# Low products ahead of high ones in every second weight block of a wide product

## The chip, the cores and the metric

The kernel runs on one core of a Trainium2 chip. The metric is the device time of one execution in microseconds; the figure before is the median of three runs. TensorE (PE) multiplies into PSUM, VectorE (DVE) and ScalarE (ACT) split weights and evacuate PSUM, GpSimd (POOL) does little here, and SyncE (SP) issues nearly all loads.

## What is computed

Two transformer-like layers run over one sequence of 256 tokens with 2048 features. The first has an adaptive normalization, four kinds of attention and a gated feed-forward part; the second has banded attention, a recurrent time mix, a cross attention on a memory, and three gated products that are merged. What matters for this change is that nearly all work is products of an activation with a large weight matrix:

```python
def first_block(x, c, ...):
    mod = c_act @ ada_w[layer] + ada_b[layer]
    u = rms_norm(h, norm_mix_g[layer]) * (1.0 + sc1) + sh1
    h = h + g1 * hybrid_mixer(u, w_in[layer], ..., w_out[layer])
    u = rms_norm(h, norm_ffn_g[layer]) * (1.0 + sc2) + sh2
    h = h + g2 * swiglu(u, ffn_w_gate[layer], ffn_w_up[layer], ffn_w_down[layer])
    return rms_norm(h, final_norm_g)

def hybrid_layer(x, mem, ...):
    proj = h @ w_in
    ...
    merged = (jax.nn.sigmoid(ga) * (ya @ w_up_a)
              + jax.nn.sigmoid(gb) * (yb @ w_up_b)
              + jax.nn.sigmoid(gc) * (yc @ w_up_c))
    return x + merged @ w_o
```

## The kernel before

A product is computed in a split form: a weight W is cast to a high part Wh, and the low part is Wl = W - Wh; an activation tile X[k] holds its high part in columns 0 to 255 and its low part in columns 256 to 511. The method `piece` loads one weight block of 128 x 1024 with a DMA on SyncE's queue (L296), casts it on ScalarE (L298) and subtracts on VectorE (L299). There are three buffers each of W, Wh and Wl.

The method `unit_b` is the feature-major product (weights are the stationary operand). A unit makes two output tiles of 128 features in two PSUM banks (`pd`, four banks in all) and walks over the K input tiles in blocks of four k, so that a block has eight weight tiles. Where the product is wide (`self.narrow` is false), a block has eight high products, Wh times both halves of X[k], 512 columns, and then eight low products, Wl times the high half of X[k], 256 columns into the first half of the same bank. The sum of the two halves of a bank is made at the end by `total` (L228 copy on ScalarE, L229 addition on VectorE). K is 16 for most products (four blocks a unit), 8 for w_out (two blocks) and 22 for ffn_w_down (six blocks, the last a half one). `narrow` is true only in the first phase, `start`, whose products have another form. `unit_a` is the token-major product, where activations are stationary; it isn't touched. All matmuls are recorded by the helper `mm` (L194), so in the profile they are told apart by their tiles: pd<-s,Wh and pd<-s,Wl are the ones spoken of.

The products are in program order, with two things interleaved: `step` advances side tasks (attention heads, the scan) after each block, and `trickle` issues pieces of the ada_w product, which VectorE computes (L457). A scheduler then orders each engine's instructions by its own estimates; the accumulations of a bank may change places in it. Phases in the profiled execution: `start` to about 200 us, the first layer's mixer to 530, its output product w_out with the last heads to 615, ffn from 630 to about 1300, the second layer behind it. In the second half of w_out the evacuation also squares the new rows (L1097 on ScalarE) and adds the squares up (L1101 on VectorE); ffn begins with a normalization by that sum.

Of the kernel before, what the change touches and what calls it, by code (L numbers as in the profile page):

```python
# [151 lines left out]
class Build:  # L152
# [158 lines left out]
    def unit_b(self, X, w, segs, evacs, row0=0, full=False):  # L311


        nb = len(evacs)
        K = len(X)
        first, part = self.parts.pop((w, tuple(segs)), (0, None))
        if part is not None:
            evacs = [self.add_part(part[:, b * 256:b * 256 + 256], evacs[b]) for b in range(nb)]
        ps = [self.pd.tile([128, 512], F32, name="pd", tag="pd") for _ in range(nb)]
        kp = 1024 // (128 * nb)  # L320
        for k0 in range(first, K, kp):
            nk = min(kp, K - k0)
            if full:
                W = self.whole(w, row0, segs, k0, nk, 128 * nb)
            else:
                Wh, Wl = self.piece(w, row0, segs, k0, nk, 128 * nb)
            tiles = [(b, k0 + j, slice(b * 128, b * 128 + 128), j) for b in range(nb) for j in range(nk)]

            for b, k, c, j in tiles:
                if full:  # L330
                    self.mm(ps[b][:, :256], W[:, j, c], X[k], k == 0, k == K - 1)
                elif self.narrow:
                    self.mm(ps[b][:, :256], Wh[:, j, c], X[k][:, :256], k == first, False)
                    self.mm(ps[b][:, :256], Wh[:, j, c], X[k][:, 256:], False, False)
                else:
                    self.mm(ps[b], Wh[:, j, c], X[k], k == first, False)
            for b, k, c, j in () if full else tiles:
                self.mm(ps[b][:, :256], Wl[:, j, c], X[k][:, :256], False, k == K - 1)
            if k0 + nk == K:
                for b in range(nb):  # L340
                    evacs[b](ps[b])
            self.trickle(self.rate)
            self.step()
# [1512 lines left out]
```

## Time and profile before

| | before |
|---|---|
| median of 3 runs | 2491.7 us (2488.88 to 2492.43) |
| profiled execution | 2491.23 us |
| its span, first to last instruction | 2489.5 us |
| mean granted TensorE clock | 0.988 of full speed |
| TensorE busy | 2417.4 us, 97% |
| VectorE busy | 1748.2 us, 70% |
| ScalarE busy | 1254.9 us, 50% |
| DMA | 527.12 MB, mean 212 GB/s |

Busy times are those of one profiled execution. A matmul's end in the profile is modelled and its row overlaps the next one, so the pace of TensorE is read from starts. A row of the timeline merges equal instructions that follow each other on one engine; its duration runs from the first start to the last modelled end.

### The profile page before, as it was taken

How to read it: one execution, taken by the hardware profiler on the slowest of the kernel's cores; microseconds unless marked ns; L12 is line 12 of the kernel's file. 1: busy time of each engine (PE TensorE's matmuls, PEld its weight loads, DVE VectorE, ACT ScalarE, POOL GpSimd, SP SyncE). 2: the span in 40 equal slices, each digit the busy share in tenths (PEclk: the TensorE clock that was granted, in tenths of full speed). 3: DMA queues.
4: the chain of work that ended last, by engine and by line, in shares of the span. 5: the costliest groups of instructions: out<-in, count | busy, mean ns of one | idle time of the engine just before them, and what ended most of it. 6: DMA issues, size and time to landing. Idle time of an engine off the chain costs nothing.

```text
span 2489.5 us, 38757 instructions
## 1 busy us (share of the span) xinstructions
PE 2417.4 (97%) x14666; PEld 2064.1 (83%) x14666; DVE 1748.2 (70%) x3321; ACT 1254.9 (50%) x2134; POOL 55.5 (2%) x102
## 2 busy tenths in 40 slices
PE   7989999998899999999999999999999999999999
PEld 5668788776788888888888877888888888888888
DVE  6677777899667755555566787778986766666664
ACT  3035446774544444444455554566564645444543
POOL 0000000000000000000000002000110000000000
PEclk9999999999899999999999999999999999999999
DMA  9988778778588866666655655335553465666665
GB/s 332 363 328 290 230 275 289 253 251 284 161 270 285 279 185 190 193 188 187 189 184 185 216 176 178 112 115 162 163 156 124 148 191 186 188 192 187 186 231 167
DMA packets 161095, 527.12 MB, mean 212 GB/s; under 512 B 22878, under 2 KB 32892, under 8 KB 160780
## 3 DMA queue, kind: packets, MB, share of 16 engines
q1 hardware_dynamic: 156892, 515.98, 63.4%
q0 software_dynamic: 4016, 8.66, 1.1%
q8 instruction: 115, 1.88, 0.3%
q14 instruction: 72, 0.59, 0.1%
HBM read 516.17 MB, written 9.45 MB: 211 GB/s over the span
## 4 chain that ended last, share of the span: by engine, by line
PE 81%; DVE 9%; DMA 6%; ACT 2%; issue 2%; SPq 0%; DVEq 0%; ACTq 0%
PE pd L194 74%; PE ps L194 7%; DVE Wl L299 3%; DMA W<-in_w_in_dram 2%; DMA b<-in_ada_w_dram 1%; ACT Wh L298 1%; DVE b L457 1%; PE ps L198 1%; DMA W<-in_w_out_dram 1%; DMA s<-in_memt_dram 0%; DVE dt L229 0%; DMA Wl<-in_w_mem_kv_dram 0%; DMA s<-in_xt_dram 0%; DMA tab<-fd 0%; DVE b L1306 0%
## 5 line engine op out<-in xcount | busy, mean ns | idle before, releaser
L194 PE MATMUL pd<-s,Wh 128*128 128x512 f32 (+1 forms) x5648 | 1423.3, 393 | 25.4 <-ACT Wh L298 11.2
L299 DVE TENSOR_TENSOR Wl<-W,Wh 128x1024 fp32r<-128x1024 f32 (+1 forms) x738 | 889.1, 1206 | 548.1 <-ACT Wh L298 526.6
L298 ACT CAST Wh<-W 128x1024 fp32r<-128x1024 f32 (+1 forms) x738 | 763.2, 1035 | 883.2 <-PE pd L194 627.2
L194 PEld LDWEIGHTS pd<-s,Wh 128*128 128x128 f32 x5648 | 1008.1, 190 | 210.6 <-ACT Wh L298 15.0
L194 PEld LDWEIGHTS pd<-s,Wl 128*128 128x128 f32 x5536 | 764.5, 191 | 72.7 <-DVE Wl L299 9.3
L194 PE MATMUL pd<-s,Wl 128*128 128x256 f32 x5536 | 793.5, 286 | 11.0 <-DMA Wl<-in_w_mem_kv_dram 5.6
L457 DVE SCALAR_TENSOR_TENSOR b<-b,tq 128x1024 f32<-128x1024 f32 x192 | 233.5, 1220 | 51.0 <-DMA b<-in_ada_w_dram 50.3
L194 PE MATMUL pd<-Wh,s 128*128 128x512 f32 (+4 forms) x496 | 141.6, 373 | 0.0
L229 DVE TENSOR_TENSOR dt<-pd,dt 128x256 f32<-128x256 f32 x289 | 110.4, 416 | 11.2 <-ACT dt L228 10.7
L228 ACT COPY dt<-pd 128x256 f32<-128x256 f32 x289 | 94.9, 371 | 24.4 <-PE pd L194 22.4
L194 PEld LDWEIGHTS pd<-Wh,s 128*128 128x128 f32 x496 | 88.4, 189 | 20.5 <-issue 11.9
L194 PE MATMUL pd<-Wl,s 128*128 128x512 f32 (+4 forms) x264 | 96.3, 386 | 0.0
L194 PE MATMUL ps<-s 64*128 64x256 f32 (+7 forms) x356 | 65.0, 364 | 4.5 <-DVE s L1612 2.5
L194 PEld LDWEIGHTS pd<-Wl,s 128*128 128x128 f32 x264 | 49.8, 189 | 14.2 <-issue 10.2
L194 PEld LDWEIGHTS ps<-s 64*128 64x128 f32 (+4 forms) x356 | 43.6, 184 | 21.2 <-issue 6.6
L194 PE MATMUL ps<-q,con 128*128 128x256 f32 x132 | 40.4, 412 | 11.3 <-ACT q L1091 4.2
L214 DVE TENSOR_TENSOR s<-q,s 128x256 fp32r<-128x256 f32 x104 | 39.8, 420 | 7.2 <-ACT s L213 6.9
L629 ACT ACTIVATE e<-e,y 128x256 f32<-128x256 f32 x80 | 35.8, 449 | 17.9 <-DVE y L627 17.7
L194 PEld LDWEIGHTS ps<-q,con 128*128 128x128 f32 x132 | 23.4, 197 | 20.3 <-ACT q L1091 4.4
L213 ACT CAST s<-q 128x256 fp32r<-128x256 f32 x104 | 37.6, 403 | 3.7 <-DVE q L1727 1.9
L636 ACT ACTIVATE e<-e,y 128x256 f32<-128x256 f32 x88 | 33.7, 447 | 4.3 <-DVE y L673 3.1
L206 ACT ACT_TABLE_LOAD x25 | 32.1, 1283 | 0.4
(295 smaller groups left out, 1381.8 us busy)
## 6 DMA issues: line engine op xcount, KB each, us to landing
W<-in_w_in_dram SPq DMA_DIRECT2D x334, 512.0 KB, 3.7
b<-in_ada_w_dram SPq DMA_DIRECT2D x192, 512.0 KB, 5.2
W<-in_ffn_w_gate_dram SPq DMA_DIRECT2D x88, 512.0 KB, 3.9
W<-in_ffn_w_up_dram SPq DMA_DIRECT2D x88, 512.0 KB, 4.4
W<-in_ffn_w_down_dram SPq DMA_DIRECT2D x80, 512.0 KB, 3.5
W<-in_w_out_dram SPq DMA_DIRECT2D x32, 512.0 KB, 4.2
W<-in_w_o_dram SPq DMA_DIRECT2D x32, 512.0 KB, 3.7
W<-in_w_up_a_dram SPq DMA_DIRECT2D x16, 512.0 KB, 3.6
```

What stands on the lines that cost most here:

```text
L194: self.nc.tensor.matmul(out, lhsT, rhs, start=start, stop=stop)
L198: self.nc.tensor.transpose(out, in_, self.ident[p0:p0 + n, p0:p0 + n])
L206: self.nc.scalar.activation(out, x, AF.Abs_reciprocal_sqrt)
L213: self.nc.scalar.copy(out[:, :256], src)
L214: self.nc.vector.tensor_tensor(out[:, 256:], src, out[:, :256], op=OP.subtract)
L228: self.nc.scalar.copy(t, ps[:, 256:512])
L229: self.nc.vector.tensor_tensor(t, ps[:, :256], t, op=OP.add)
L298: nc.scalar.copy(Wh[:, :n], W[:, :n])
L299: nc.vector.tensor_tensor(Wl[:, :n], W[:, :n], Wh[:, :n], op=OP.subtract)
L457: nc.vector.scalar_tensor_tensor(W, W, 1.0, self.crow[half], op0=OP.mult, op1=OP.mult, accum_out=acc[:, k:k + 1])
L629: nc.scalar.activation(e[:, lo:hi], e[:, lo:hi], AF.Exp, bias=nm[:, a:a + 1], accum_out=sm[:, a:a + 1])
L636: self.nc.scalar.activation(e[:, lo:hi], e[:, lo:hi], AF.Copy, scale=f[:, a:a + 1])
```

## The change

In a wide unit, the blocks are counted from the first one; in every second of them (the second, the fourth and so on) the low products are recorded ahead of the high ones. The flag that ends an accumulation moves with the last product. The first block of a unit stays as it was, so the flag that starts an accumulation stays with a high product. The same products are made with the same operands. The program order of a unit with four blocks becomes high, low, low, high, high, low, low, high, and the next unit begins with high.

```diff
+            swap = (k0 - first) // kp % 2 == 1 and not full and not self.narrow
+            if swap:
+                for b, k, c, j in tiles:
+                    self.mm(ps[b][:, :256], Wl[:, j, c], X[k][:, :256], False, False)
             for b, k, c, j in tiles:
                 if full:
                     self.mm(ps[b][:, :256], W[:, j, c], X[k], k == 0, k == K - 1)
...
                 else:
-                    self.mm(ps[b], Wh[:, j, c], X[k], k == first, False)
-            for b, k, c, j in () if full else tiles:
+                    self.mm(ps[b], Wh[:, j, c], X[k], k == first, swap and k == K - 1)
+            for b, k, c, j in () if full or swap else tiles:
                 self.mm(ps[b][:, :256], Wl[:, j, c], X[k][:, :256], False, k == K - 1)
```

The scheduler makes other orders of it. On TensorE in the mixer, ahead of the side products 7x128 of the first attention heads, the difference of the two orders reads as follows (pd are the unit's banks, s the activation tiles, ps the side tasks' banks):

```order
 L194 MATMUL pd<-s,Wl 128x256 x8
 L194 MATMUL pd<-s,Wh 128x512 x8
-L194 MATMUL pd<-s,Wl 128x256 x8
-L194 MATMUL pd<-s,Wh 128x512 x8
-L194 MATMUL pd<-s,Wl 128x256 x8
-L194 MATMUL pd<-s,Wh 128x512 x8
-L194 MATMUL pd<-s,Wl 128x256 x5
+L194 MATMUL pd<-s,Wl 128x256 x16
+L194 MATMUL pd<-s,Wh 128x512 x14
 L194 MATMUL ps<-s,y 7x128
```

The runs of eight have become runs of 16, and the side products now cut a run of high products instead of a run of low ones.

On VectorE in the second half of w_out, before the change (Wl the split, dt the addition of a bank's halves, s_389 and its neighbours the updated rows, b2 the ada pieces, s_5516 the sum of squares):

```order
L299 TENSOR_TENSOR Wl_5726<-W_5724,Wh_5725 128x1024
L229 TENSOR_TENSOR dt_5707<-pd_5658,dt_5707 128x256
L229 TENSOR_TENSOR dt_5713<-pd_5659,dt_5713 128x256
L1076 SCALAR_TENSOR_TENSOR s_389<-dt_5707,mod_87,s_389 128x256
L1076 SCALAR_TENSOR_TENSOR s_389<-dt_5713,mod_87,s_389 128x256
L457 SCALAR_TENSOR_TENSOR b2_5746,y_5617<-b2_5746,tq_88 128x1024
L299 TENSOR_TENSOR Wl_5751<-W_5749,Wh_5750 128x1024
L1101 TENSOR_TENSOR s_5516<-s_5516,s_5711 128x512
L457 SCALAR_TENSOR_TENSOR b2_5783,y_5617<-b2_5783,tq_88 128x1024
L299 TENSOR_TENSOR Wl_5790<-W_5788,Wh_5789 128x1024
```

The same stretch of VectorE after the change (line numbers behind the edit are five higher):

```order
L299 TENSOR_TENSOR Wl_5726<-W_5724,Wh_5725 128x1024
L229 TENSOR_TENSOR dt_5707<-pd_5658,dt_5707 128x256
L462 SCALAR_TENSOR_TENSOR b2_5746,y_5617<-b2_5746,tq_88 128x1024
L1081 SCALAR_TENSOR_TENSOR s_389<-dt_5707,mod_87,s_389 128x256
L229 TENSOR_TENSOR dt_5713<-pd_5659,dt_5713 128x256
L299 TENSOR_TENSOR Wl_5751<-W_5749,Wh_5750 128x1024
L1081 SCALAR_TENSOR_TENSOR s_389<-dt_5713,mod_87,s_389 128x256
L462 SCALAR_TENSOR_TENSOR b2_5783,y_5617<-b2_5783,tq_88 128x1024
L1106 TENSOR_TENSOR s_5516<-s_5516,s_5711 128x512
L299 TENSOR_TENSOR Wl_5790<-W_5788,Wh_5789 128x1024
```

The second addition and update now stand behind an ada piece and on both sides of the next split, and the sum of squares stands one ada piece later.

On TensorE at the end of w_out, before the change (ps<-s,con are the products of the sum of squares):

```order
L194 MATMUL pd<-s,Wh 128x512 x16
L194 MATMUL pd<-s,Wl 128x256 x16
L194 MATMUL pd<-s,Wh 128x512 x8
L194 MATMUL pd<-s,Wl 128x256 x5
L194 MATMUL ps<-s,con 128x256 x2
L194 MATMUL pd<-s,Wl 128x256 x3
L194 MATMUL ps<-q,con 128x256 x2
```

The same place on TensorE after the change:

```order
L194 MATMUL pd<-s,Wl 128x256 x8
L194 MATMUL pd<-s,Wh 128x512 x8
L194 MATMUL pd<-s,Wl 128x256 x16
L194 MATMUL pd<-s,Wh 128x512 x8
L194 MATMUL ps<-s,con 128x256 x2
L194 MATMUL ps<-q,con 128x256 x2
```

The last weight block's high products now stand behind its low ones, and the side products have moved behind both.

## Rows read from the trace of the kernel before

**Rows 1.** The page's busy shares, then TensorE's groups by line and form.

```profile
PE 2417.4 (97%) x14666; PEld 2064.1 (83%) x14666; DVE 1748.2 (70%) x3321; ACT 1254.9 (50%) x2134; POOL 55.5 (2%) x102
...
L194 PE MATMUL pd<-s,Wh 128*128 128x512 f32 x5344 | 1372.2, 397 | 11.7 <-DVE s L214 10.3 <-DVE s L239 0.6 <-ACT Wh L298 0.3
L194 PE MATMUL pd<-s,Wl 128*128 128x256 f32 x5536 | 793.5, 286 | 11.0 <-DMA Wl<-in_w_mem_kv_dram 5.6 <-DVE Wl L299 5.4
```

**Rows 2.** Windows: length, busy time of each engine, granted clock, DMA, by stage.

```profile
530.00:650.00 120.00, 96.13 (x476) 77.31 (x476) 107.88 (x229) 71.37 (x140) 0.00 (x0) 0.89 0.69 230
650.00:1300.00 650.00, 650.00 (x3724) 571.70 (x3723) 401.03 (x537) 307.87 (x449) 0.00 (x0) 1.00 0.67 215
1300.00:2000.00 700.00, 689.22 (x4945) 588.70 (x4944) 539.30 (x1149) 391.23 (x660) 44.60 (x78) 1.00 0.51 158
```

**Rows 3.** Waits of TensorE for Wl: whole span, then 530 to 650 us.

```profile
PE pd L194 <- DVE Wl L299: 5.4, 8, 1.6
...
PE pd L194 <- DVE Wl L299: 4.8, 7, 1.6
```

**Rows 4.** Timeline of TensorE in ffn (start, duration, engine, line, operation, count).

```profile
1201.94 2.00 PE L194 MATMUL pd<-s,Wh 128*128 128x512 f32 x8
1203.79 1.11 PE L194 MATMUL pd<-s,Wl 128*128 128x256 f32 x8
1204.74 0.63 PE L194 MATMUL pd<-s,Wh 128*128 128x512 f32 x2
```

**Rows 5.** Timeline of TensorE at 551 us, a run of 16 high products.

```profile
551.60 3.82 PE L194 MATMUL pd<-s,Wh 128*128 128x512 f32 x16
```

**Rows 6.** Timeline of TensorE from 1204.43 us: the last four of a low run.

```profile
1204.26 0.64 PE L194 MATMUL pd<-s,Wl 128*128 128x256 f32 x4
```

**Rows 7.** Timeline in ffn: a split (VectorE) and the block that uses it.

```profile
1009.53 1.22 DVE L299 TENSOR_TENSOR Wl<-W,Wh 128x1024 fp32r<-128x1024 f32 x1 [1.29 <-ACT Wh L298]
...
1016.63 0.64 PE L194 MATMUL pd<-s,Wl 128*128 128x256 f32 x4
```

**Rows 8.** Timeline of TensorE with side work between runs, 1674 to 1678 us.

```profile
1674.63 1.20 PE L194 MATMUL pd<-s,Wl 128*128 128x256 f32 x8
1675.67 1.02 PE L194 MATMUL ps<-s,con 128*128 128x256 f32 x4
1676.34 2.19 PE L194 MATMUL pd<-s,Wh 128*128 128x512 f32 x8
1678.37 0.88 PE L194 MATMUL pd<-s,Wl 128*128 128x256 f32 x6
```

**Rows 9.** Timeline in the second half of w_out, one unit.

```profile
598.79 1.22 DVE L299 TENSOR_TENSOR Wl<-W,Wh 128x1024 fp32r<-128x1024 f32 x1
...
600.06 1.21 PE L194 MATMUL pd<-s,Wl 128*128 128x256 f32 x8 [0.37 <-DVE Wl L299]
...
600.84 0.85 ACT L228 COPY dt<-pd 128x256 f32<-128x256 f32 x2 [0.17 <-PE pd L194]
...
602.21 0.75 DVE L229 TENSOR_TENSOR dt<-pd,dt 128x256 f32<-128x256 f32 x2
...
602.87 0.87 DVE L1076 SCALAR_TENSOR_TENSOR s<-dt,mod,s 128x256 f32<-128x256 f32 x2
...
603.73 1.22 DVE L457 SCALAR_TENSOR_TENSOR b<-b,tq 128x1024 f32<-128x1024 f32 x1
...
605.36 0.72 ACT L1097 ACTIVATE s<-s 128x256 f32<-128x256 f32 x2
...
606.11 0.69 DVE L1101 TENSOR_TENSOR s<-s 128x512 f32<-128x512 f32 x1 [1.08 <-ACT s L1097]
606.72 1.22 DVE L299 TENSOR_TENSOR Wl<-W,Wh 128x1024 fp32r<-128x1024 f32 x1
```

**Rows 10.** Timeline at the end of w_out.

```profile
612.92 1.22 DVE L299 TENSOR_TENSOR Wl<-W,Wh 128x1024 fp32r<-128x1024 f32 x1
...
615.58 0.70 PE L194 MATMUL pd<-s,Wl 128*128 128x256 f32 x3
```

## The prediction

> **What bounds the kernel now.** I read first the page's busy shares and the groups by line. TensorE is busy for 97% of the span, and the wide high products (5344 matmuls of 512 columns in wide blocks, written H here) and the low products (256 columns, L) are its two largest groups [rows 1]. A busy TensorE is modelled, so I read the stages next. From 650 to 1300 us TensorE has no idle time at all, from 1300 to 2000 it lacks 11 us of 700, but from 530 to 650 it is busy for 96 of 120 us while VectorE is busy for 108 [rows 2]. So there are two regimes. Where TensorE issues without a gap, the time is the sum of the distances from one matmul's start to the next. From 530 to 650 the loop of weight load, split and evacuation sets the pace, and seven of TensorE's waits there, 4.8 us, end with the low half Wl of a weight block [rows 3].
>
> The pace inside a regular block is in the timeline of 1202 to 1205 us: eight H take 1.85 us from the first start to the first L, eight L 0.95 us to the next H, a block 2.80 us [rows 4]. In one place the scheduler already put two blocks' H side by side: a run of 16 H shows 3.82 us against 2.00 us for a run of 8. Both figures end with the same modelled last matmul, so the second eight cost 1.82 us, 0.03 less than the eight that follow an L [rows 4, 5]. For L I compare the halves of a run: starts at 1203.79, 1204.26 and 1204.74, so 0.47 us for the first four and 0.48 for the last four [rows 4, 6]. The first L after an H are a little cheap, the first H after an L a little dear; neither is a pause that a join would remove whole.
>
> **The change part by part.** *Count of matmuls, weight loads, splits, DMAs:* the same, no cost. 337 of the 676 wide blocks stand the other way round.
>
> *H runs joined.* Counted over the two instruction orders, an H run follows directly on an L 608 times before and 349 times after. In 530 to 650 us, where TensorE isn't the bound, the count goes from 22 to 25; elsewhere 262 such places go. At 0.03 us each: -7.9 us. The rows are rounded to 0.01, so 0.02 to 0.04, -5.2 to -10.5 us.
>
> *L runs joined.* An L run follows directly on an H 666 times before, 344 after; 321 of the lost places lie outside 530 to 650 us. Each takes the cheap first four with it: 0.01 us each, +3.2 us (bounds 0 and 0.02 by rounding, 0 to +6.4). Net of the two: **-4.7 us**; with all bounds against each other -10.5 to +1.2.
>
> These joins are pace, and nothing else is late there: from 650 to 1300 us the first L of a block starts at 1016.63 us while its Wl was ready at 1009.53 + 1.22 = 1010.75, 5.9 us earlier [rows 7]. In a swapped block L starts 1.85 us sooner, and the Wh buffer of a swapped block is freed 0.95 us later, because its H stand last; the later cast and subtraction behind that eat into the same cushion, and it stays above 3 us. On SyncE's queue the weight DMAs wait for the subtraction that frees W, which moves by the same 0.95 us; the loads of ada_w between them keep their order. VectorE and ScalarE lose nothing there.
>
> *Side work between the runs.* Attention and scan matmuls cut runs about as often as before (179 runs of side work before, 181 after), but at other points: H after side work 118 to 87 times, L after it 32 to 65 times. The rows price one entry: eight H after side work take 1676.34 to 1678.37, 2.03 us against 1.85, so +0.18; eight L take 1674.63 to 1675.67, 1.04 against 0.95, so +0.09 [rows 4, 8]. That would be 31 x 0.18 less 33 x 0.09 = -2.6 us; but the side matmul ahead of an L may pay its part, which these rows don't separate, and the number of cuts is equal, so the other end is 0. I take **-1.0 us**, nearer to none.
>
> *Waits on Wl outside 530 to 650 us.* Only 0.6 us of the 5.4 us that TensorE waits for Wl lies there [rows 3]. A swapped block near scan or attention work may find Wl late by up to 1.85 us. Bounds: 0, and as much again as the 4.8 us of the other stretch; I take **+0.5 us**, since the plain blocks there hardly wait.
>
> *530 to 650 us, product w_out.* A unit has two blocks, and the second is now L before H. In the timeline Wl of a second block is ready at 600.01, its L run, the copies and additions follow, the squares stand at 605.36, their sum at 606.11, and the next unit's Wl starts at 606.72, 7.93 us after the one at 598.79 [rows 9]. Before, H was done while TensorE waited; after, it stands between Wl and the evacuation. The chain from Wl to the next such Wl is then L 0.95 + H 1.85 + copy 0.43 (half of the pair) + additions 0.75 + updates 0.87 + squares 0.72 + sum 0.69 + split 1.22 = 7.48 us without hand-overs: just under the loop of 7.93 us that is there now. The order on VectorE fills the later wait with an ada product ahead of the additions. So I take **+1.0 us** for some units that miss; bounds 0 and 12 (below). The last unit has nothing behind it to hide in: its Wl is ready at 612.92 + 1.22 = 614.14, and its last L ends at 615.58 + 0.70 = 616.28, because four side products stand between; that is 2.1 us, and after the change it is 0.95 us of L and a run of eight H, 2.00 us with its end, 2.95 us in all [rows 4, 10]. ffn's normalization waits for that: **+0.8 us**.
>
> *Sum:* -4.7 - 1.0 + 0.5 + 1.0 + 0.8 = **-3.4 us**. Against the profiled execution (2491.2 us, its span 2489.5) that is 2487.8 us; the profiled execution is 0.5 us under the median of 2491.7.
>
> **The rivals.** *The order of matmuls is free.* If the 0.03 us of rows 4 and 5 belongs to that one place, joining brings nothing: -1.0 + 2.3 gives 2492.5 us. For it: the rows show one clean run of 16 H and none of 16 L at full pace. Against it: H and L pace differ by position in the same run. The Trainium skill's page "TensorE: Matmul & The Clock Gate", section "Back-to-back issue gap", gives a warm distance of N / 2.4 + 2.5 ns, which depends on the columns alone; by it a block would be 8 x 216 + 8 x 109 ns = 2.6 us in any order, and the change would do nothing. The trace doesn't agree on the level (2.80 us) and shows 1.85 and 1.82 us for the same eight matmuls.
>
> *More comes of it.* With 0.04 us per H join, nothing lost at L, the full price of the side entries and no new waits: -10.5 - 2.6 = -13 us, 2478 us; the middle of this case is 2482.
>
> *Slower: w_out's loop takes the H in.* If an ada product (1.22 us) stands ahead of the additions and the squares follow it, the chain is 8.7 us against 7.93, 0.8 us more in each of 16 units, +12.4 us: 2491.2 - 5.7 + 0.5 + 0.8 + 12.4 = 2499 us. It decides from about 0.6 us per unit, where it outweighs the 3.4 + 1.0 us and another 5. For it: VectorE's 90% in that stretch. Against it: the additions there could already start late, behind a whole product and a split.
>
> **How the numbers follow.** Forecast 0.45 (2485 to 2490), free order 0.22 (2490 to 2494), more 0.19 (below 2485), slower loop 0.14 (above 2494). Below 2481.5 lies about half of the third, above 2496.5 some two thirds of the fourth: the range is 2481.5 to 2496.5. A measurement of this kernel tells about 0.2%, 5 us, from no change. Faster by more (below 2486.7): the third and a third of the forecast, 0.35. Slower by more: 0.09 of the fourth and a little for what I don't see, 0.11. The same: 0.54. So the likeliest outcome is a small gain at the edge of what can be told.
>
> **What would show it.** In the ffn stage a pair of blocks should take 2 x 2.80 less 0.02 us, a run of 16 H 3.82 us and a run of 16 L 0.96 us more than one of 8. From 650 to 1300 us TensorE should stay without idle time. From 530 to 650 us the stretch should last within 3 us of before; if it grows by 10, the slower rival holds. The prediction is wrong in its main term if a pair of blocks isn't shorter, or is shorter by over 0.05 us.

## The result and the profile after

The changed kernel takes 2511.2 us (median of 5 runs, 2506.7 to 2519.3), against 2491.7 us before: a ratio of 1.0085, 95% interval 1.0071 to 1.01. It is slower by 19.5 us. The prediction had a gain, 2487.8 us, with a range from 2481.5 to 2496.5: wrong in sign and in size. The profiled execution took 2508.21 us (span 2506.4).

The page after the change, busy shares and chain, then TensorE's two large groups by line and form (busy, mean ns, idle time ahead of them and its releasers); they answer to [rows 1]:

```profile
PE 2419.7 (97%) x14666; PEld 2065.0 (82%) x14666; DVE 1778.4 (71%) x3321; ACT 1260.3 (50%) x2134; POOL 55.6 (2%) x102
...
PE 66%; issue 11%; DMA 10%; DVE 9%; ACT 3%; POOL 1%; SPq 0%; DVEq 0%; ACTq 0%; POOLq 0%
...
L194 PE MATMUL pd<-s,Wh 128*128 128x512 f32 x5344 | 1316.0, 395 | 23.1 <-ACT Wh L298 13.2 <-DVE s L214 9.7 <-DVE s L239 0.2
L194 PE MATMUL pd<-s,Wl 128*128 128x256 f32 x5536 | 754.9, 287 | 17.7 <-DVE Wl L299 12.7 <-DVE q L568 2.9 <-ACT s L213 1.8
```

The joins worked: the high products are busy for 56 us less and the low ones for 39 us less, but a busy time counts the modelled ends, which fall away when runs are joined, so this is no gain in time; TensorE's busy time as a whole is 2.3 us longer. What is new is idle time: 13.2 us ahead of the high products that ended with the cast to Wh, 0.3 before, and 12.7 us ahead of the low ones that ended with Wl, 5.4 before.

The windows of the changed kernel by stage (length, busy time of each engine, granted clock, DMA share, GB/s), against [rows 2]. The stage from 650 to 1300 us is cut in three; the last two rows are the kernel before in two of the three parts:

```profile
530.00:650.00 120.00, 91.37 (x475) 73.91 (x474) 110.67 (x233) 70.71 (x139) 0.00 (x0) 0.93 0.68 227
650.00:740.00 90.00, 90.00 (x518) 79.50 (x517) 59.44 (x79) 45.26 (x67) 0.00 (x0) 1.00 0.73 234
740.00:905.00 165.00, 156.54 (x872) 133.35 (x871) 115.08 (x171) 72.61 (x110) 0.00 (x0) 1.00 0.74 252
905.00:1300.00 395.00, 395.00 (x2276) 349.24 (x2275) 226.24 (x280) 187.08 (x267) 0.00 (x0) 1.00 0.62 190
1300.00:2000.00 700.00, 688.44 (x4926) 587.00 (x4925) 538.03 (x1136) 388.98 (x653) 44.70 (x78) 1.00 0.51 157
...
740.00:905.00 165.00, 165.00 (x948) 145.26 (x947) 120.28 (x174) 77.78 (x114) 0.00 (x0) 1.00 0.77 261
905.00:1300.00 395.00, 395.00 (x2263) 347.26 (x2262) 220.08 (x281) 186.03 (x270) 0.00 (x0) 1.00 0.61 189
```

From 740 to 905 us TensorE now lacks 8.5 us, in a stretch where it had lacked none. That is the gate and up products of ffn's first half, and it is the part of ffn beside which most of the last 32 pieces of ada_w run: their products start from 700 to 889 us, 25 of them behind 740.

To place the loss I compare the start of the n-th high product in two traces; the number of such products is the same in every version, so the difference is how far one kernel lags behind the other. In a swapped block the high products come last, so this reading moves by up to 1 us with the place in a unit; where the order of runs differs, as at 527 us, it jumps. The changed kernel lags by 1.7 us at 422 us (time of before), 4.3 to 7.0 at 527, 4.6 at 685, 4.8 at 741, **16.9 at 908**, 15.7 at 1244 and 18.3 at the end, where the two spans differ by 16.9. Twelve of the 18 us arise between 741 and 908, some 3 to 5 between 422 and 685 (where runs scatter by as much), and in the rest of ffn the lag shrinks.

What the engines wait for from 740 to 905 us (us in total, times, longest), first before, then after:

```profile
ACT Wh L298 <- PE pd L194: 66.1, 42, 2.1
DVE Wl L299 <- ACT Wh L298: 34.1, 37, 2.2
...
DVE b L457 <- DMA b<-in_ada_w_dram: 8.0, 10, 1.5
```

```profile
ACT q L1141 <- DVE dt L229: 30.6, 7, 5.0
DVE b L462 <- DMA b<-in_ada_w_dram: 28.4, 13, 2.6
ACT Wh L298 <- DMA W<-in_ffn_w_gate_dram: 22.4, 11, 2.8
...
ACT Wh L298 <- DMA W<-in_ffn_w_up_dram: 14.4, 6, 2.6
```

Before, the cast (L298) waited for TensorE to free a Wh buffer: the supply of weights was ahead of TensorE. After, it waits for weight loads, and VectorE for loads of ada_w: the supply is behind. What reaches TensorE of this, in the same stretch of the changed kernel:

```profile
PE pd L194 <- ACT Wh L298: 4.5, 5, 1.2
...
PE pd L194 <- DVE Wl L299: 3.7, 7, 0.6
```

**The round.** The timeline of the changed kernel shows how that closes on itself (start, duration, engine, line, operation, in brackets the idle time ahead and its end):

```profile
784.64 0.42 SPq L201 DMA_DIRECT2D b<-in_ada_w_dram  x1
...
790.84 1.23 DVE L462 SCALAR_TENSOR_TENSOR b<-b,tq 128x1024 f32<-128x1024 f32 x1 [2.38 <-DMA b<-in_ada_w_dram]
...
792.00 0.42 DVE L229 TENSOR_TENSOR dt<-pd,dt 128x256 f32<-128x256 f32 x1
...
792.45 0.42 ACT L1141 ACTIVATE q<-dt 128x256 f32<-128x256 f32 x1 [4.70 <-DVE dt L229]
...
792.77 1.03 ACT L298 CAST Wh<-W 128x1024 fp32r<-128x1024 f32 x1
...
793.83 2.49 DVE L299 TENSOR_TENSOR Wl<-W,Wh 128x1024 fp32r<-128x1024 f32 x2 [0.82 <-ACT Wh L298]
...
793.86 2.14 PE L194 MATMUL pd<-s,Wh 128*128 128x512 f32 x8 [0.96 <-ACT Wh L298]
...
795.09 1.59 SPq L296 DMA_DIRECT2D W<-in_ffn_w_gate_dram  x2
...
796.73 0.43 SPq L201 DMA_DIRECT2D b<-in_ada_w_dram  x1
```

A load of ada_w leaves SyncE at 784.64, behind weight loads; it lands 6.2 us later, and the ada product starts at 790.84. Behind it VectorE has the addition of the gate, for which ScalarE's silu waits (4.70 us); behind the silu stands the cast, behind the cast the two subtractions Wl, and only these free two W buffers, so that SyncE can issue the two weight loads at 795.09 and, behind them, a load of ada_w at 796.73. Another one had left at 788.87, so a round holds two pieces. One round is 796.73 - 784.64 = 12.09 us and feeds four blocks, for which TensorE needs 4 x 2.79 = 11.16 us. Over 24 pieces in the middle of the stretch (718 to 852 us before, 724 to 869 after) two pieces take 12.13 us, against 11.16 before. The lag grows from 741 to 867 us (time of before), which is 126 / 11.16 = 11.3 rounds; 11.3 x 0.97 = 11 us of the 11.9 that it grows by.

The same piece of work in the kernel before:

```profile
779.18 1.23 DVE L457 SCALAR_TENSOR_TENSOR b<-b,tq 128x1024 f32<-128x1024 f32 x1 [0.30 <-DMA b<-in_ada_w_dram]
...
780.75 1.23 DVE L299 TENSOR_TENSOR Wl<-W,Wh 128x1024 fp32r<-128x1024 f32 x1
...
781.89 0.75 DVE L229 TENSOR_TENSOR dt<-pd,dt 128x256 f32<-128x256 f32 x2
...
782.00 3.32 SPq L296 DMA_DIRECT2D W<-in_ffn_w_gate_dram  x2
782.35 0.42 ACT L1136 ACTIVATE q<-dt 128x256 f32<-128x256 f32 x1 [1.43 <-DVE dt L229]
```

Here a subtraction stands between product and additions, and a W buffer is free (load at 782.00) before the silu has run. The scheduler had changed VectorE's order with the swap: from product, split, addition, addition to product, addition, addition, split, split. SyncE's order, two weight loads and one of ada_w in turn, is the same in both.

### The profile page after: what moved, and what is told of

Read it like the earlier page. It is cut to its first block, busy times and chain, and to the rows that moved or that the text cites. A ratio compares the mean times of both kernels' runs of the same rounds, so it can differ in the third digit from the quotient of the medians.

```text
span 2506.4 us, 38715 instructions
## 1 busy us (share of the span) xinstructions
PE 2419.7 (97%) x14666; PEld 2065.0 (82%) x14666; DVE 1778.4 (71%) x3321; ACT 1260.3 (50%) x2134; POOL 55.6 (2%) x102
## 4 chain that ended last, share of the span: by engine, by line
PE 66%; issue 11%; DMA 10%; DVE 9%; ACT 3%; POOL 1%; SPq 0%; DVEq 0%; ACTq 0%; POOLq 0%
PE pd L194 61%; DMA b<-in_ada_w_dram 5%; PE ps L194 4%; DVE Wl L299 3%; DMA W<-in_w_in_dram 2%; DVE b L462 2%; ACT Wh L298 1%; DMA W<-in_w_out_dram 1%; PE ps L198 1%; DVE dt L229 0%; DVE q L1354 0%; DVE s L214 0%; POOL tq L1367 0%; DMA q<-rd 0%; DMA s<-in_memt_dram 0%
## 5 line engine op out<-in xcount | busy, mean ns | idle before, releaser
L194 PE MATMUL pd<-s,Wh 128*128 128x512 f32 (+1 forms) x5648 | 1368.2, 392 | 37.0 <-ACT Wh L298 23.8
L194 PEld LDWEIGHTS pd<-s,Wh 128*128 128x128 f32 x5648 | 1029.1, 190 | 237.6 <-ACT Wh L298 29.2
L298 ACT CAST Wh<-W 128x1024 fp32r<-128x1024 f32 (+1 forms) x738 | 762.3, 1036 | 603.7 <-PE pd L194 431.0
L194 PEld LDWEIGHTS pd<-s,Wl 128*128 128x128 f32 x5536 | 723.9, 192 | 59.3 <-DVE Wl L299 20.3
L194 PE MATMUL pd<-s,Wl 128*128 128x256 f32 x5536 | 754.9, 287 | 17.7 <-DVE Wl L299 12.7
L228 ACT COPY dt<-pd 128x256 f32<-128x256 f32 x289 | 105.8, 370 | 247.9 <-PE pd L194 246.2
L229 DVE TENSOR_TENSOR dt<-pd,dt 128x256 f32<-128x256 f32 x289 | 120.8, 422 | 92.2 <-ACT dt L228 89.8
L194 PEld LDWEIGHTS pd<-Wh,s 128*128 128x128 f32 x496 | 88.1, 188 | 20.1 <-issue 11.3
L242 ACT ACTIVATE dt<-pd 128x256 f32<-128x256 f32 x64 | 24.3, 383 | 63.4 <-PE pd L194 58.5
L634 ACT ACTIVATE e<-e,y 128x256 f32<-128x256 f32 x80 | 35.8, 449 | 19.9 <-DVE y L632 19.8
L1141 ACT ACTIVATE q<-dt 128x256 f32<-128x256 f32 x44 | 18.3, 417 | 39.0 <-DVE dt L229 39.0
```

The costliest lines, as they stand in the source:

```text
L194: self.nc.tensor.matmul(out, lhsT, rhs, start=start, stop=stop)
L228: self.nc.scalar.copy(t, ps[:, 256:512])
L229: self.nc.vector.tensor_tensor(t, ps[:, :256], t, op=OP.add)
L242: nc.scalar.activation(t, ps[:, 256:512], AF.Copy, scale=scale)
L298: nc.scalar.copy(Wh[:, :n], W[:, :n])
L634: nc.scalar.activation(e[:, lo:hi], e[:, lo:hi], AF.Exp, bias=nm[:, a:a + 1], accum_out=sm[:, a:a + 1])
```

## The experiments

The lag that each run gains between 741 and 908 us against the kernel before (n-th high product, profiled execution), and its comparison with before from several runs:

| run | swapped where, and what else | gained 741 to 908 | median, us | ratio to before, 95% |
|---|---|---|---|---|
| after | all wide products | +12.1 | 2511.2 | 1.0085 (1.0071 to 1.01) |
| x1 | all but ffn beside ada | +3.4 | 2497.9 | 1.003 (1.0016 to 1.0045) |
| x2 | only ffn beside ada | +12.0 | 2500.9 | 1.0038 (1.0022 to 1.0055) |
| x3 | all; ada load one piece early | +7.6 | 2509.8 | 1.0072 (1.005 to 1.0094) |
| x4 | all; no ada load in ffn | -0.6 | 2499.1 | 1.0029 (1.0015 to 1.0042) |
| x5 | only where no ada is pending | -0.1 | 2489.5 | 0.9997 (0.9986 to 1.0008) |
| x6 | only first layer's w_in, w_out | 0.0 | 2498.8 | 1.0032 (1.002 to 1.0045) |
| x8 | all; ada load two pieces early | +12.1 | 2509.4 | 1.007 (1.0053 to 1.0088) |
| x9 | all; four W buffers | -0.6 | 2487.1 | 0.9982 (0.9973 to 0.9991) |
| x10 | none; four W buffers | 0.0 | 2488.0 | 0.9989 (0.9979 to 0.9998) |
| x11 | all; ada pieces one block later | -0.6 | 2498.4 | 1.0036 (1.0023 to 1.0048) |
| x12 | all; ada loads by GpSimd | -0.6 | 2505.4 | 1.0064 (1.0045 to 1.0082) |
| x13 | all; x9's small pools, three W | +12.4 | 2514.5 | 1.0098 (1.0075 to 1.012) |
| x14 | only first layer's w_in | 0.0 | 2494.5 | 1.0031 (1.002 to 1.0043) |
| x15 | only w_out | 0.0 | 2493.1 | 1.0018 (1.0002 to 1.0035) |
| x16 | all but w_in, w_out; four W | -0.6 | 2484.5 | 0.9991 (0.9982 to 0.9999) |

The runs of before beside them had medians of 2491.0 us (x1 to x4), 2490.9 (x5 to x9), 2490.8 (x10 to x13) and 2488.7 (x14 to x16). The ratio isn't the quotient of two medians; the two differ by up to 0.0008.

**Where it is lost: x1 and x2.** The first line is x1's, the second x2's; `bg` holds the pieces that are pending.

```diff
+            swap = swap and not (self.stage == "ffn" and self.rate > 0 and self.bg)
...
+            swap = swap and bool(self.stage == "ffn" and self.rate > 0 and self.bg)
```

x1: 

> The changed kernel with the low products ahead everywhere but in the blocks of ffn that are recorded while pieces of ada_w are still to come (some 60 blocks, 733 to 885 us). Theory A (the loss of 12 us arises only there, where VectorE stands still behind an ada piece whose load comes late): the 12 us go, 2508 - 12 = 2496 to 2499 us, and ffn runs without idle time on TensorE. Rival B (the loss is a matter of the whole kernel, the shorter cushion of the low halves): no more than 2 or 3 us come back, 2506 us or more.

x2: 

> The reverse: the kernel before, with the low products ahead only in the blocks of ffn beside the pending ada_w pieces. Theory A: 2491.7 + 12 = 2503 us, all of the gain in time between 735 and 890 us. Rival B: within 3 us of 2491.7.

Measured: without the swap beside the pieces some 13 us come back; with the swap there alone 10 us are lost, all 12.0 us of its trace between 741 and 908. The loss needs swapped blocks and pieces of ada_w in the same place. A short cushion everywhere is out: in the changed kernel, whose blocks are swapped there too, the lag doesn't grow from 908 to 1244 us. x1 is 7 us from before, so something is lost elsewhere too. Of these 7 us it still loses 3.4 in the same stretch. It has the order of before there (product, split, two additions), and yet its cast waits 43.8 us for loads of the gate's and the up product's weights, against 2.8 before. So the order isn't all that can put the supply behind. That x1 comes into the stretch 6.7 us late doesn't explain it: x6 and x11 come 5.3 and 7.7 us late and lose nothing. What does it in x1 is open.

**Is it the loads: x4, x3 and x8.** x4 multiplies a tile that is there already in place of a loaded one, so it leaves the modulation's chunks 20 to 23 out. x3 and x8 keep a queue of loads issued ahead; `lead` is 2 in x3 and 3 in x8. First x4's lines, then those of x3 and x8.

```diff
+        if self.stage == "ffn":
+            A = self.crow[1 - half]
...
+        while len(self.loaded) < self.lead and self.coming:
+            self.loaded.append(self.ada_load(*self.coming.popleft()))
+        W = self.loaded.popleft()
```

x4: 

> The changed kernel, whose ada_w pieces in ffn load nothing: the product on VectorE stays, on a tile that is there already (so the modulation of chunks 20 to 23 is left out of the result). Theory A: no wait for the loads, the 12 us go, 2496 us, or 1 to 2 less since 16 MB of traffic go. Rival C: 2506 us or more.

x3: 

> The changed kernel, with the load of each ada_w piece in ffn issued one piece (two weight blocks, 5.6 us) ahead of its use. Same work. Theory A: VectorE's wait for these loads goes from 28 us between 740 and 930 us to nearly 0, and the stretch loses its 12 us: about 2497 us. Rival C (what costs is the place of the ada products and of the paired splits on VectorE, not their load): VectorE no longer waits for a load, but the time stays within 3 us of 2508.

x8: 

> The changed kernel; in the feed-forward products each load of ada_w is issued two pieces ahead of its product (one piece ahead had left the load 5 to 6.6 us in front of its product, hardly more than in the changed kernel). Theory of the closed round: four blocks cannot go faster than load of ada_w behind two weight loads (6.2 us), product (1.2), the two additions, silu and cast behind it (1.9), and the two subtractions that free two W buffers (2.5), 12.1 us against 11.1 of TensorE. With the load two pieces ahead the product waits for nothing, the round is open, and 8 to 12 of the 12 us between 745 and 905 come back: about 2500 us, no wait of VectorE for ada_w over 1 us. Rival, the transfers themselves are too slow when they come in threes: the waits move to the weights, and it stays at 2509 us.

x4 gives the 12 us back, but less can be concluded than was expected of it: with nothing to load, the products ran early as well, in front of 740 us, so it takes the whole of ada_w out of the stretch. x3 and x8 give nothing sure back (the 7.6 of x3 is from the shortest of its seven executions), and they don't test what they were made for: in both a load still leaves SyncE 5.0 to 7.6 us ahead of its product, with medians of 6.6 and 6.7, as in the changed kernel (5.1 to 7.6, median 6.6). The scheduler put it back behind the weight loads. (The four terms that x8's expectation names add up to 11.8 us and not to 12.1; in the rows of the round the last of them, up to the load at 796.73, is 2.9 us.) Whether a load that is really earlier would help isn't known from them.

**Where no piece is pending: x5.**

```diff
+            swap = swap and not self.bg
```

> The blocks are swapped only where no piece of ada_w is pending any more: in the feed-forward product from about 885 us on, and in the second layer; the mixer and the first half of the gate and up products stand as before. By the theory that the loss arises where pieces of ada_w run beside swapped blocks, only the joins are left: 1.3 us less from 930 to 1300, 1.3 us less after 2058, against 0 to 4 us that were lost between 1300 and 2000: 2488 to 2492 us, no difference that can be told. By the rival of a cushion that is too short everywhere it is 2495 us or more.

2489.5 us, no difference that can be told. So where no piece of ada_w is pending the swap as a whole costs nothing that can be seen. In its trace that is a small gain less a small loss: 1.4 us come back from 930 to 1300 and 1.3 behind 2058, and from 1300 to 2058 the lag grows by 1.4.

**Opening the round: x9, with x10 and x13 as controls, and x11.** The first six lines are the pools: x9 has them on the changed kernel, x10 on the kernel before, x13 all but the first pair on the changed kernel. The last pair is x11, which has the pools of the changed kernel.

```diff
-WB = {"W": 3, "Wh": 3, "Wl": 3}
+WB = {"W": 4, "Wh": 3, "Wl": 3}
-BUFS = {"q": 12, "dt": 6, "e": 8, "pt": 4, "tab": 3, "b2": 3, "tq": 1}
+BUFS = {"q": 10, "dt": 6, "e": 8, "pt": 3, "tab": 3, "b2": 3, "tq": 1}
-        self.yp = P("tiny", 32)
+        self.yp = P("tiny", 24)
...
-                    self.rate = 0.5
+                    self.rate, self.credit = 0.5, 0.0
```

x9: 

> The changed kernel with a fourth buffer for W (and, to make room, 10 instead of 12 of q, 3 instead of 4 of pt, 24 instead of 32 of the tiny ones). By the theory of the closed round the loads no longer have to wait for the subtraction of the block just ahead, so the load of ada_w behind them goes out some 2.8 us earlier and the round is open: 745 to 905 loses at most 3 of its 12 us, about 2500 us. If the transfers themselves are the limit, the fourth buffer changes nothing: 2509 us. The smaller pools may cost some us in the mixer, which the lag by matmul separates.

x13: 

> The changed kernel with the smaller pools of x9 but three W buffers: control for x9. By every theory that names the fourth W buffer as the cure it stays at 2508 to 2514 us; if it were the pools that changed the order of work, it would come to 2487 us.

x10: 

> The kernel before with the pools of x9 (four W buffers, smaller q, pt and tiny). If the fourth buffer only undoes what the swap cost, before gains nothing by it: 2489 to 2493 us, and the swap on top of it is worth the 3 to 5 us of the joins (x9 2487.1). If the buffer is worth something by itself, also without the swap, this one comes to 2484 to 2487 us and the swap is worth nothing.

x11: 

> The changed kernel with three W buffers; in the feed-forward products the pieces of ada_w come behind the second block of each pair (the swapped one) and not behind the first. In the program VectorE then has a split between each product and the additions of the gate (product, split, addition), and split and product take turns, where the changed kernel has product, two additions, two splits. By the theory of the closed round it is this order that holds W's buffers back: 745 to 905 then loses at most 4 of its 12 us, 2499 to 2503 us. If three buffers are too few for any order of swapped blocks, it stays at 2508 to 2512 us.

With a fourth W buffer the changed kernel takes 2487.1 us, 13 us less than was expected: the 19.5 us are gone, and not only the 12 of ffn. The smaller pools alone (x13) bring the changed kernel nothing. In ffn the two numbers that tell the cases apart are TensorE's busy time from 740 to 905 us and what the cast waits for. x9:

```profile
740.00:905.00 165.00, 165.00 (x951) 145.86 (x950) 120.75 (x171) 78.08 (x114) 0.00 (x0) 1.00 0.77 261
...
ACT Wh L298 <- PE pd L194: 44.7, 29, 3.1
...
DVE b L462 <- DMA b<-in_ada_w_dram: 6.5, 6, 2.5
```

TensorE lacks nothing, and the cast waits for TensorE again. x10 is the kernel before with the same pools; the same stretch and VectorE's wait for ada_w there:

```profile
740.00:905.00 165.00, 165.00 (x946) 145.12 (x946) 117.85 (x171) 77.21 (x114) 0.00 (x0) 1.00 0.77 259
...
DVE b L457 <- DMA b<-in_ada_w_dram: 23.0, 18, 2.4
```

The wait is nearly as long as the 28.4 us of the changed kernel, and TensorE still has no idle time in x10. So VectorE's wait for ada_w alone costs nothing; it costs when the freeing of W hangs on it. The fourth buffer, with the smaller pools, brings the kernel before 2.8 us (0.11%, interval 0.02 to 0.21), and the swap on top of it nothing that can be told: 0.9982 and 0.9989 overlap.

x11 leaves three buffers and everything else, and only moves the pieces of ada_w by one block, from behind the first block of a pair to behind the swapped one. Its timeline:

```profile
783.44 1.23 DVE L299 TENSOR_TENSOR Wl<-W,Wh 128x1024 fp32r<-128x1024 f32 x1 [1.17 <-ACT Wh L298]
...
784.59 1.22 DVE L462 SCALAR_TENSOR_TENSOR b<-b,tq 128x1024 f32<-128x1024 f32 x1
...
785.73 1.22 DVE L299 TENSOR_TENSOR Wl<-W,Wh 128x1024 fp32r<-128x1024 f32 x1
...
787.37 0.42 DVE L229 TENSOR_TENSOR dt<-pd,dt 128x256 f32<-128x256 f32 x1 [0.42 <-ACT dt L228]
```

Split and product take turns, a split stands between the product and the addition, the product waits for nothing, and the 12 us of the stretch are gone (2498.4 us, 12.8 less than the changed kernel). So it is neither the swap as such nor three buffers as such, but the order in which product, additions, splits and loads met. What of x11's gain is VectorE's order and what is the other place of the load between the weight loads isn't separated; both moved by one block.

**Another queue: x12.**

```diff
+        if self.stage == "ffn":
+            nc.gpsimd.dma_start(W, src)
```

> The changed kernel; in the feed-forward products the loads of ada_w are issued by GpSimd and no longer stand in SyncE's queue behind the weight loads that wait for a W buffer. The loads x3 and x8 meant to move kept their place in that queue (6 to 7.5 us ahead of their product, behind the weights of three blocks on); here they can go as soon as a buffer of theirs is free. If the queue is what makes them late, VectorE no longer waits for ada_w and 8 us or more of the 12 come back, 2499 to 2503 us. If the transfers as such are too many at once, the waits for the weights grow and it stays at 2508 us or more.

Off SyncE's queue the 32 pieces ran bunched from 635 to 734 us, so that none is left beside 740 to 905. The windows of x12, first ahead of that stretch and then in it, and last the kernel before ahead of it:

```profile
655.00:740.00 85.00, 78.91 (x441) 67.35 (x440) 72.19 (x116) 38.13 (x56) 12.91 (x24) 1.00 0.90 321
740.00:905.00 165.00, 165.00 (x948) 145.69 (x947) 97.16 (x122) 81.30 (x121) 0.00 (x0) 1.00 0.63 193
...
655.00:740.00 85.00, 85.00 (x487) 74.72 (x486) 57.42 (x81) 41.32 (x63) 0.00 (x0) 1.00 0.77 248
```

Here far more is moved (DMA share 0.90, 321 GB/s, against 0.77 and 248 before), TensorE lacks 6.1 us, and the run loses 6 us; that the transfers themselves are the limit is likely, but not shown. It doesn't answer the question of the queue.

**The other 7 us: x6, x14, x15 and x16,** a line each in this order; x16 has x9's pools besides.

```diff
+            swap = swap and self.stage == "mixer"
...
+            swap = swap and self.stage == "mixer" and w == "w_in"
...
+            swap = swap and w == "w_out"
...
+            swap = swap and self.stage != "mixer"
```

x6: 

> The swap in the mixer's products alone (up to the end of w_out, about 650 us). The lag of the changed kernel was +7 us at 530 us and +4.6 at 685. If the mixer really loses by the swap, 2495 to 2498 us; if the lag there is only the scatter between runs and is caught up in the w_out loop, 2490 to 2492 us.

x14: 

> Swapped blocks only in the first layer's w_in product (the feature-major pairs from about 330 to 575 us). x6, swapped from 330 to 650 us, lost 7.8 us. If the mixer's part of it costs most, this run is at 2495 to 2498 us; if it is the w_out loop, at 2489 to 2492 us.

x15: 

> Swapped blocks only in the w_out loop (about 575 to 650 us). The rival of the prediction, that this loop takes the blocks in one by one and waits for the earlier low part, had it 10 us longer: 2499 to 2501 us. If the mixer ahead of it costs most, 2490 to 2493 us. If each costs half, both this run and x14 are at 2494 to 2496 us.

x16: 

> x9 (four W buffers, smaller q, pt and tiny), with the blocks of w_in and w_out of the first layer not swapped. With the round open in the feed-forward product and no swap in the mixer, only the joins are left: 3 us less than the kernel before with the same pools (2488.0), 2484 to 2486 us. If the fourth buffer had cured the mixer too, it would be no better than x9, 2487 us.

The first layer's mixer loses 7.8 us by the swap (x6, interval 5.0 to 11.2). Alone, w_in loses 5.8 and w_out 4.4 us by the medians, 7.7 (5.0 to 10.7) and 4.5 (0.5 to 8.7) by the ratios. So w_in costs something for sure, w_out probably; how the 7.8 us divide can't be told. In the traces this is no single wait. In x6 TensorE waits from 422 to 575 us 3.8 us for Wl and 3.0 for Wh in four waits, where before it waited 0.5 for Wl. But x9, which isn't slower, waits 6.4 us for Wl there, so these waits aren't shown to be the cost:

```profile
PE pd L194 <- DVE Wl L299: 3.8, 2, 2.1
PE pd L194 <- ACT Wh L298: 3.0, 2, 2.1
```

The lag from 422 to 685 us grows by -1.0 to +4.0 us in the runs with neither product swapped (x2, x5, x10, x16) and +1.3 to +8.6 in those with both (x9's +1.3 becomes -3.9 if it is read one product later), so the trace of one execution can't give the place closer. x16 is 2484.5 us with a ratio of 0.9991; it can't be told from x9 or x10. So there is no sign that the mixer still costs much with four buffers, but also no proof.

The best version by its ratio is x9, the swap with a fourth W buffer: 0.18% faster than before (0.09 to 0.27). Of that, x10 has 0.11% without the swap.

## Why the prediction was wrong

*Pace of the joins, -4.7 us: right in kind and size where it can be seen.* TensorE in ffn after the change:

```profile
1200.10 2.08 PE L194 MATMUL pd<-s,Wl 128*128 128x256 f32 x16
1202.01 3.82 PE L194 MATMUL pd<-s,Wh 128*128 128x512 f32 x16
1205.66 2.08 PE L194 MATMUL pd<-s,Wl 128*128 128x256 f32 x16
```

The runs of 16 high products show the 3.82 us that was named, and 16 low ones show 2.08, 0.97 more than the 1.11 of eight [rows 4] (0.96 was named). From 964 to 1244 us, 50 pairs of blocks, the lag shrinks from 16.7 to 15.7: 0.02 us a pair, as predicted; it does so in each of the runs that swap there (1.0 us, x1, x3 to x5, x8, x9, x11 to x13, x16) and in none of the others (0.0, x2, x6, x10, x14, x15). From 930 to 1300 and from 2058 to 2490 together that is 2.6 us. In between it is lost again: from 1300 to 2058 the lag grows by 1.4 to 5.6 us in the eleven runs that swap there, by -0.5 to 2.0 in the five others. Starts lie 3.65 / 16 = 0.228 us apart for high products and 1.91 / 16 = 0.119 for low ones. By the formula in the Trainium skill's page "TensorE: Matmul & The Clock Gate", section "Back-to-back issue gap", it would be an estimated 216 and 109 ns, whatever the order; the page gives the formula for an isolated matmul, which the prediction left out. The trace has more than that. The first two distances of a high run behind low products are longer, 0.233 and 0.236 us where later ones are 0.227, and the first one of a low run behind high products is shorter, 0.113 where later ones are 0.120 (medians from 950 to 1240 us, the same in both kernels). So the rival of a free order fell, and the gain that it denied is real and small.

*Nothing late from 650 to 1300 us, and waits outside 530 to 650 us at +0.5 us with a bound of 4.8: the step that failed.* It stood on the sentences that "nothing else is late there", that the cushion "stays above 3 us" and that "VectorE and ScalarE lose nothing there", read from one place, 1009 us [rows 7]. There it holds: from 905 to 1300 us TensorE has no idle time after the change. But the windows of [rows 2] put 650 to 1300 us into one row, and in its first part the pieces of ada_w run: DMA share 0.77 from 740 to 905 against 0.61 behind it in the kernel before, and ten waits of VectorE for them, 8.0 us. There the supply of weights was only just ahead. The prediction named SyncE's queue and the loads of ada_w in it and was right that they keep their order; it didn't ask what order the scheduler would give VectorE there. It had compared the two orders on VectorE only in w_out. Cost: 12 us. There is a smaller case of the same step from 1800 to 1900 us: the lag grows there by some 2 to 4 us in every run that swaps in the second layer and by at most 0.6 in the others. The changed kernel has two waits there that the kernel before has not:

```profile
PE pd L194 <- DVE Wl L299: 1.5, 1, 1.5
PE ps L194 <- DMA s<-mk_d: 1.2, 1, 1.2
```

These two take back what the joins bring; why they arise was not tested.

*530 to 650 us, w_out, +1.0, and the slower rival with +12.4 there: neither.* The lag goes from 4.3 or 7.0 at 527 to 5.6 us at 650, either way within the 3 us that were named, and no unit-by-unit loss of 0.8 us is seen. What w_out costs alone (x15, 4.4 us, interval 0.5 to 8.7) is below the rival's price; in the whole change it comes on top of a mixer that is late already, and part of it may fall into waits that were there before. The chance for slower, 0.11, was on the wrong mechanism.

*Ahead of 530 us* the prediction had no term but the joins, the side work's -1.0 and a share of the +0.5 for waits. x14 shows +5.8 us for w_in, which runs up to about 575 us; which wait makes it stays open. The entry prices of rows 8 can't be checked against that; a gain from side work isn't visible anywhere.

*End of w_out, +0.8:* not separable from the rest of the mixer.

In sum: 12 us in ffn beside ada_w, shown by x1, x2, x9 and x11; 5 to 11 us in w_in and w_out, shown by x6 without a wait as its cause; some 3 us back by the joins, and as much lost in the second layer.

## What to carry to other kernels

Where buffers in a ring are freed by an engine that also does other work in program order, write down the round, from the load over each engine's queue to the load that its end sets free, and compare it with the pace of the engine it feeds, in the stretch where the most other traffic shares it and not in a quiet one. A change that only reorders the consumer can make a scheduler reorder the producers; compare the orders of all engines in every kind of stretch, not only where a wait is known. One buffer more, or the other work shifted by one block, may be worth more than the change.

## What had not been expected of the hardware

Equal 512 KB loads took longer to land at nearly the same mean rate: those of ada_w from 740 to 905 us whose landing the trace gives took a median of 4.5 us before (five loads) and 6.1 us after (six), while the rate went from 261 to 252 GB/s. In x10 they took 6.2 us (five loads) at 259 GB/s, and that cost nothing. What sets this time was not tested. Order mattered at the hundredth: eight high products behind eight of the same kind take 0.03 us less than behind low ones, and 2.6 of the 4.7 us that the joins promised can be seen in the trace, though not in the time.
